# A decoder step on one core: the recorder's rule for a side step of TensorE also looks at the two dense halves behind it

## The chip, the cores and the metric

One core of a Trainium2 chip runs the whole program. The metric is the device time of one execution in microseconds (us); shorter is better. Of the kernel before there are three timed runs and one profiled execution.

## The reference

One layer of a hybrid decoder runs over a prompt of 512 tokens and over 8 samples of 4 tokens each, 544 columns in all, which share the weights (D = 1024, fp32 in and out).

```
z = rmsnorm(x) @ w_in                      # q, k, v of 8 attention heads; q, f, i, gate of 4 HGRN2 heads
att = dilated_attention(q, [cache; k], [cache; v]);  att = head_rmsnorm(att)
f = lb + (1 - lb) * sigmoid(hf)            # HGRN2: S_t = diag(f_t) S_{t-1} + (1 - f_t) outer i_t
o = head_rmsnorm(S_t^T silu(hq)) * silu(hg)
x += [att, o] @ w_out
x += cross_attention(rmsnorm(x), memory_k, memory_v) @ w_co
x += (silu(conv3(rmsnorm(x) @ w_gate)) * (rmsnorm(x) @ w_up)) @ w_down
y = rmsnorm(x)                             # outputs: y, new k and v, HGRN2 states, conv rows, memory k and v
```

## The kernel before

Activations lie transposed in SBUF, 128 features by 544 columns. Each fp32 product of a weight with the activations is made of three products of rounded parts (type fp32r): high by high, high by low, low by high. A **dense half** is one such product for 128 output rows and either 256 or 288 columns: 8 contraction tiles by 3 products, 24 matmuls into one bank of PSUM. In the names, `ps_hf_0` is the half of 256 columns of the projection hf (the forget gate of an HGRN2 head) and `ps_hf_256` the half of 288.

Between the dense halves stands smaller work, mostly in plain fp32, each matmul of which shows in the trace as two records: prompt attention (`psS`, `psT`, `psO`), the samples' attention over the cached window (`psd`, `psdo`), and HGRN2 (`psA`, `psB`, `psL`, `psin`, `psu`, `psU`, `pso`). A step `psdo` multiplies probabilities by a tile `st` of 512 KB of cached values, four matmuls at a time; five such tiles stand in SBUF and SyncE's DMA queue refills each as it comes free. Many matmuls of HGRN2 are only 32 by 32.

The program is not issued as it is written. The class `Tape` records every instruction, joins those of TensorE into steps, and the function `order` then plays the steps through with assumed durations and decides the order on every engine. On TensorE the dense halves are **main** steps in a fixed order. All else there is a **side** step, which may go between two main steps once its inputs are there. When a main step is ready too, a side step must pass two tests: the function `held_back`, which returns how long the step would wait for TensorE's own instructions, must give under 0.1 us, and the array must stay busy enough (`ACTIVE`, `SPELL`). When no main step is ready the tests are not made.

`held_back` and `fetch` carry the recorder's picture of the instruction stream. Instructions come to TensorE in blocks of 256 (`BLOCK`). A variable `codes` counts them. A block counts as asked for when TensorE is 64 instructions short of the end of the block two before it, and as there after 4.3 us (`FETCH`) plus up to 2.2 us for what the DMA queue still holds (`bus`). A matmul of type fp32r counts as 2 instructions and one of fp32 as 4. The other engines' order comes from the same play, so when a TensorE step moves, its inputs' and outputs' instructions and the loads that wait for its buffers move with it.

All instructions of the program that the recorder issues carry one line number, L719 (L691 for DMAs), so the profile is read by the names of tiles.

Of the kernel before, what the change touches and what calls it, by code (L numbers as in the profile page):

```python
# [260 lines left out]
class Tape:  # L261
# [201 lines left out]
    def order(self, before=None):  # L463
# [25 lines left out]
        now, clock, bus, todo, done, burst, first = 0.0, [0.0, 0.0], 0.0, len(self.steps), [], False, None  # L489
# [5 lines left out]
        codes, fetched, heard = self.AHEAD_OF, {0: 0.0, 1: 0.0}, dict.fromkeys(waiting, -1)  # L495

        def hears(s):

            news = {}
            for d in s.deps:  # L500
                if d.engine != "PE" and d.nth > heard[d.engine]:
                    news[d.engine] = max(news.get(d.engine, -1), d.nth)
            return news

        def held_back(s):

            block, wait = (codes + s.codes + len(hears(s)) // 2 - 1) // self.BLOCK, 0.0
            for b in range((codes - 1) // self.BLOCK + 1, block + 1):
                share = (b * self.BLOCK - codes) / s.codes
                at = now + wait + share * s.length  # L510
                wait += max(0.0, fetched.get(b, at + self.FETCH) - at)
            return wait

        def fetch(s, wait):
            nonlocal codes
            news = hears(s)
            codes += len(news) // 2
            heard.update(news)
            for b in range((codes - 1) // self.BLOCK + 1, (codes + s.codes - 1) // self.BLOCK + 1):
                fetched.setdefault(b + 1, now + wait + self.FETCH)  # L520
            for b in range((codes + 63) // self.BLOCK + 1, (codes + s.codes + 63) // self.BLOCK + 1):
                share = max(0.0, (b * self.BLOCK - codes - 64) / s.codes)
                fetched[b + 1] = now + share * (wait + s.length) + self.FETCH + min(2.2, max(0.0, bus - now - 0.5))
            codes += s.codes

        ran, cold, mode = [], [0.0, -10.0], (128, 128)
# [1 line left out]
        def active(at):  # L528

            done = 0.0  # L530
            for a, b, work in reversed(ran):
                if b <= at - self.SPELL:
                    break
                done += work * (b - max(a, at - self.SPELL)) / (b - a)
            return done
# [8 lines left out]
        def fits(s):  # L544
            want = needs(s)
            return all(room[k] >= v for k, v in want.items()) and ("a" not in want or leaves_room(s, want["a"]))
# [18 lines left out]
        def start(s):  # L565
# [9 lines left out]
            if s.bytes:  # L575
                free[s.engine] = now + (0.9 if s.engine == "POOL" else 0.4)
                bus = max(bus, now) + s.bytes / 300e3
                s.end = bus + (3.6 if s.engine == "POOL" else 2.2)
            else:
                held_up = max(0.0, port[s.engine == "DVE"] - now) if s.port else 0.0  # L580
                if s.port:
                    port[s.engine == "POOL"] = now + held_up + s.length
                if s.engine == "PE":
                    held_up = held_back(s) + self.SWITCH * (s.mode != mode)
                    fetch(s, held_up)
                    mode = s.left_in
                    if now > 12.0 and now > cold[1] and active(now) < self.IDLE * self.SPELL:
                        cold[:] = cold[0] + self.COLD, now + 2 * self.SPELL
                    ran.append((now, now + held_up + s.length, s.work))
                free[s.engine] = s.end = now + held_up + s.length  # L590
# [26 lines left out]
        while todo:  # L617
            for f in [f for f in frees if f[0] <= now + 1e-9]:
                room[f[1]] += 1
                frees.remove(f)  # L620
            moved = False
            for e in ("SP", "ACT", "DVE", "POOL"):
                if free[e] <= now + 1e-9:
                    at = clock[0] + min(now - clock[1], 4.0)
                    can = [s for s in waiting[e] if s.ready <= now + 1e-9 and s.begin <= at + (s.lead or self.LEAD) and fits(s)]
                    if can:
                        busy = port[e == "DVE"] > now + 0.1
                        start(min(can, key=lambda s: (s.begin + 2.0 * (s.port and busy), s.number)))
                        moved = True
            if free["PE"] <= now + 1e-9:  # L630
                can = [s for s in waiting["PE"] if s.ready <= now + 1e-9 and fits(s)]
                main = [s for s in can if s.main]
                side = [s for s in can if not s.main]
                if main:
                    side = [s for s in side if held_back(s) < 0.1
                            and active(now + s.length) + s.work >= self.ACTIVE * self.SPELL]
                if side and first is None:
                    first = now
                even = [s for s in side if s.mode == s.left_in == mode == (128, 128)]
                if side and (burst or even or not main or sum(s.length for s in side) >= self.BURST  # L640
                             or now - first > self.PATIENCE
                             or min(s.begin for s in side) < clock[0] + now - clock[1]):
                    s = min(side, key=lambda s: (s.begin + self.NEAR * (s.mode != mode), s.number))
                    if not burst and even and main and sum(s.length for s in side) < self.BURST:
                        s = min(even, key=lambda s: (s.begin, s.number))
                    else:
                        burst, first = True, None
                    start(s)
                    moved = True
                elif main:  # L650
                    start(main[0])
                    if before is not None and now > before[nth[main[0]]] + self.BEHIND:
                        return None
                    burst = False
# [1896 lines left out]
```

## Time and profile before

| what | value |
|---|---|
| three timed runs | 823.06, 824.0 and 825.23 us; the median is 824.0 |
| the profiled execution's own time | 824.86 us |
| its span, first to last instruction | 823.1 us, so 1.76 us lie around it |
| mean granted TensorE clock | 0.993 of full speed |
| VectorE, ScalarE, GpSimd busy | 594.2, 420.8 and 157.0 us |
| bytes moved by DMA | 137.04 MB, 166 GB/s over the span |

The profile names engines by PE (TensorE's matmuls), PEld (its weight loads), DVE (VectorE), ACT (ScalarE), POOL (GpSimd) and SP (SyncE, here only a DMA queue). In the timeline view each row has the start, the time to the end of the last record, the tiles, the part of the array in use (rows*columns), the shape of what is read and how many records were merged. In a view by windows, each row is a stretch of time with the busy time of each engine and its number of instructions, then the granted clock, the busy share of the DMA engines and GB/s. Matmuls overlap in the array, so the pace is read from one start to the next and not from the length of one.

### The profile page before, as it was taken

To read this page: it belongs to the slowest core of one execution; us is meant where nothing else is said; L and a number is where in the kernel's file an instruction comes from. 1 tells how busy PE (TensorE), PEld (TensorE's weight loads), DVE (VectorE), ACT (ScalarE), POOL (GpSimd) and SP (SyncE) were. 2 spreads that over 40 slices of the span, in tenths; PEclk is the share of its full clock that TensorE was granted. 3 is DMA by queue.
4 is the path that set the end of the run, shared out by engine and by line. 5 is a ranking of instruction groups with operands and counts; after the bars stand their busy time and mean duration, and the time that the engine had idled before them with its cause. 6 is when DMAs were issued, how large, how long until landed. Compare 5 with 4: busy or idle time off the path is not lost.

```text
span 823.1 us, 18827 instructions
## 1 busy us (share of the span) xinstructions
PE 809.8 (98%) x7545; PEld 762.9 (93%) x7545; DVE 594.2 (72%) x1252; ACT 420.8 (51%) x838; POOL 157.0 (19%) x246
## 2 busy tenths in 40 slices
PE   9999999989999999999999999999999999999996
PEld 9998988868898879999889999999999999999995
DVE  6775534855778995664579999877677767978983
ACT  8412534514636835453455565654554545666553
POOL 1130000110120220232133351022011212221023
PEclk9999999989999999999999999999999999999999
DMA  9657779676863535253543265556555645776603
GB/s 319 204 143 234 251 228 312 224 252 195 291 190 103 187 105 182 70 147 105 189 157 113 65 172 138 132 150 168 129 129 151 156 135 133 183 186 172 149 3 109
DMA packets 93639, 137.04 MB, mean 166 GB/s; under 512 B 6512, under 2 KB 60656, under 8 KB 93552
## 3 DMA queue, kind: packets, MB, share of 16 engines
q1 hardware_dynamic: 86496, 123.77, 47.2%
q0 software_dynamic: 6336, 11.54, 8.9%
q8 instruction: 59, 0.97, 0.5%
q10 hardware_dynamic: 720, 0.53, 0.2%
q14 instruction: 28, 0.23, 0.1%
HBM read 127.75 MB, written 8.07 MB: 165 GB/s over the span
## 4 chain that ended last, share of the span: by engine, by line
PE 95%; ACT 2%; DMA 1%; DVE 1%; issue 1%; DVEq 0%; ACTq 0%
PE ps_d L719 9%; PE ps_au L719 7%; PE ps_ag L719 7%; PE ps_wo L719 6%; PE ps_cu L719 4%; PE ps_cg L719 3%; PE ps_k L719 3%; PE ps_q L719 3%; PE ps_g L719 3%; PE ps_cq L719 3%; PE ps_first L719 3%; PE ps_dz L719 3%; PE ps_hv L719 3%; PE ps_co L719 3%; PE ps_az L719 2%; PE ps_hf L719 2%
## 5 line engine op out<-in xcount | busy, mean ns | idle before, releaser
L719 ACT CAST wh<-wr 128x1024 fp32r<-128x1024 f32 (+1 forms) x68 | 59.0, 883 | 104.1 <-PE ps_q L719 15.4
L719 DVE TENSOR_TENSOR wl<-wr,wh 128x1024 fp32r<-128x1024 f32 (+1 forms) x68 | 70.9, 1057 | 7.8 <-ACT wh L719 7.5
L719 POOL TENSOR_TENSOR hG<-hG,hf 128x256 f32<-128x256 f32 (+1 forms) x28 | 24.7, 882 | 185.9 <-DVE hf L719 80.6
L719 POOL COPY last<-ug 128x2 f32<-128x2 f32 (+1 forms) x44 | 21.9, 520 | 125.2 <-DVE ug L719 104.6
L719 DVE TENSOR_TENSOR xr<-xr,ps_d 128x256 f32<-128x256 f32 (+1 forms) x48 | 20.9, 436 | 29.7 <-PE ps_d L719 29.5
L719 DVE SCALAR_TENSOR_TENSOR cv<-ug,vec,cv 128x560 f32<-128x560 f32 x44 | 35.1, 799 | 3.6 <-ACT cv L719 3.1
L719 POOL COPY ug<-conv_state 128x16 f32<-128x16 f32 x22 | 20.7, 941 | 17.6 <-PE ps_au L719 9.3
L719 POOL TENSOR_TENSOR acc_cx<-acc_cx,sq_cx 128x256 f32<-128x256 f32 (+1 forms) x14 | 11.7, 838 | 64.2 <-ACT sq_cx L719 64.1
L719 ACT ACTIVATE cv<-cv 128x560 f32<-128x560 f32 x22 | 14.8, 673 | 17.6 <-DVE cv L719 17.6
L719 ACT ACTIVATE P<-P,mx 128x128 f32<-128x128 f32 (+3 forms) x32 | 17.6, 554 | 9.6 <-DVE mx L719 9.5
L719 ACT ACTIVATE cv<-ug,vec 128x560 f32<-128x560 f32 x22 | 18.9, 857 | 4.6 <-DVE ug L719 3.4
L719 PE MATMUL ps_co<-coh,wh 128*128 128x256 f32 (+1 forms) x64 | 19.2, 300 | 0.1
L719 PE MATMUL ps_co<-coh,wl 128*128 128x256 f32 (+1 forms) x64 | 18.4, 288 | 0.0
L719 PE MATMUL ps_co<-col,wh 128*128 128x256 f32 (+1 forms) x64 | 18.4, 288 | 0.0
L691 POOL DMA_DIRECT2D S1u<-in_w_up x10 | 8.8, 879 | 49.6 <-DVE cv L719 25.6
L719 DVE TENSOR_TENSOR xr<-xr,ps_wo 128x256 f32<-128x256 f32 (+1 forms) x16 | 6.8, 435 | 15.5 <-PE ps_wo L719 15.5
L719 DVE TENSOR_TENSOR up<-ps_cu,keptu 128x272 f32<-128x272 f32 x20 | 8.7, 437 | 11.9 <-PE ps_cu L719 11.6
L719 PE MATMUL psdo<-st,dpt 128*32 128x256 f32 x224 | 16.4, 410 | 0.1
L719 PE MATMUL psd<-st,qbd_win 128*32 128x224 f32 x256 | 15.5, 357 | 0.0
L719 POOL TENSOR_TENSOR acc_ux<-acc_ux,sq_ux 128x256 f32<-128x256 f32 (+1 forms) x13 | 11.3, 870 | 20.4 <-ACT sq_ux L719 20.2
L719 DVE TENSOR_TENSOR hf<-ps_hf,r_mix 128x256 f32<-128x256 f32 (+1 forms) x6 | 2.6, 442 | 17.2 <-PE ps_hf L719 17.2
L719 DVE CUSTOM_DVE_ANT_0 P<-psS,bias 128x128 f32<-128x128 f32 (+3 forms) x32 | 14.3, 485 | 1.0 <-PE psS L719 1.0
(2610 smaller groups left out, 3610.5 us busy)
## 6 DMA issues: line engine op xcount, KB each, us to landing
st<-in_kwT SPq DMA_DIRECT2D x32, 448.0 KB, 5.7
st<-in_vw SPq DMA_DIRECT2D x28, 512.0 KB, 6.4
wr<-in_w_in SPq DMA_DIRECT2D x25, 512.0 KB, 4.9
wd<-in_w_down SPq DMA_DIRECT2D x24, 256.0 KB, 3.0
wru<-in_w_up SPq DMA_DIRECT2D x10, 512.0 KB, 5.4
wrg<-in_w_gate SPq DMA_DIRECT2D x9, 512.0 KB, 4.9
st<-in_mkT SPq DMA_DIRECT2D x8, 512.0 KB, 5.7
wr<-in_w_out SPq DMA_DIRECT2D x8, 512.0 KB, 3.6
```

The source lines that it names most:

```text
L691: return tape.put(engine, lambda: call(*args, **kw), outs, ins, 0.1, 0.3, size)
L719: return tape.put(engine, lambda: call(*args, **kw), outs, ins, length, lag, size, port, codes, work, mode)
```

## The change

The recorder's test of a side step becomes a look further ahead. `held_back` takes a number of instructions that follow the step; with 96, which is two dense halves of 48, a side step is held back when the blocks that it and the next two halves need would come too late. The function also works out for each block when it would be asked for, if it has not been asked for yet, and adds the queue of the DMA engines, which until now only `fetch` did.

```
-        def held_back(s):
-
-            block, wait = (codes + s.codes + len(hears(s)) // 2 - 1) // self.BLOCK, 0.0
+        def held_back(s, after=0):
+
+            block, wait = (codes + s.codes + len(hears(s)) // 2 + after - 1) // self.BLOCK, 0.0
             for b in range((codes - 1) // self.BLOCK + 1, block + 1):
-                share = (b * self.BLOCK - codes) / s.codes
+                share = min(1.0, (b * self.BLOCK - codes) / s.codes)
+                asked = now + max(0.0, ((b - 1) * self.BLOCK - 64 - codes) / s.codes) * s.length
                 at = now + wait + share * s.length
-                wait += max(0.0, fetched.get(b, at + self.FETCH) - at)
+                wait += max(0.0, fetched.get(b, asked + self.FETCH + queued()) - at)
             return wait
+
+        def queued():
+            return min(2.2, max(0.0, bus - now - 0.5))
...
                 if main:
-                    side = [s for s in side if held_back(s) < 0.1
+                    side = [s for s in side if held_back(s, 96) < 0.1
                             and active(now + s.length) + s.work >= self.ACTIVE * self.SPELL]
```

`fetch` calls `queued()` in place of the same expression. The same 7,545 matmul records are issued in the same number of instructions; helper lines move down by four (L719 becomes L723, L691 becomes L695). The order on TensorE is the same up to its row 1003 of 5,575 and again from the first halves of `ps_wo`, the output projection, on; between them lies the stretch that took from 162 to 321 us in the trace.

The first place is on TensorE, just ahead of the half `ps_hf_0` of the second HGRN2 head. Before, `psB` and `psA` (products of 32 by 32), a step `psdo` and `pst_v` (transposes of v) stand there:

```order
L719 MATMUL psB_378<-hq_343,hk_375 32x32 x17
L719 MATMUL psB_378<-kq_1_376 32x32 x17
L719 MATMUL psB_378<-kq_2_377 32x32 x17
L719 MATMUL psA_381<-kq_4_379 32x32 x16
L719 MATMUL psdo_429<-st_491,dpt_425 32x256 x4
L719 MATMUL psA_381<-kq_8_380 32x32 x16
L719 MATMUL psS_436<-cs,v_413 32x128
L719 MATMUL pst_v_430<-cs,v_413 128x128 x4
L719 MATMUL ps_hf_0_481<-xm0h,wh_479 128x256
```

On the same engine at the same place, the changed kernel has:

```order
L723 MATMUL psB_378<-hq_343,hk_375 32x32 x17
L723 MATMUL psB_378<-kq_1_376 32x32 x17
L723 MATMUL psB_378<-kq_2_377 32x32 x17
L723 MATMUL psA_381<-kq_4_379 32x32 x16
L723 MATMUL psS_436<-cs,v_413 32x128
L723 MATMUL pst_v_430<-cs,v_413 128x128 x4
L723 MATMUL ps_hf_0_481<-xm0h,wh_479 128x256
```

One step `psdo` (4 matmuls) and the step `psA` of `kq_8` (16 matmuls) have left the place.

The second place is on TensorE at the end of `ps_hf_0`. Before, side steps follow its last matmul, and `ps_hf_256` comes some 60 rows later:

```order
L719 MATMUL ps_hf_0_481<-xm7h,wl_480 128x256
L719 MATMUL psdo_429<-st_492,dpt_427 32x256 x4
L719 MATMUL psdo_429<-st_494,dpt_427 32x256 x4
L719 MATMUL psdo_429<-st_495,dpt_427 32x256 x4
L719 MATMUL psdo_429<-st_501,dpt_427 32x256 x4
L719 MATMUL psA_381<-kq_16_385 32x32 x16
L719 MATMUL psA_381<-cs,hv_362 32x128 x2
L719 MATMUL psdo_429<-st_503,dpt_427 32x256 x4
L719 MATMUL psL_388<-kq_32_386 32x32 x8
```

Now the 24 matmuls of `ps_hf_256` follow `ps_hf_0` at once, and on TensorE the side steps stand behind them:

```order
L723 MATMUL ps_hf_256_484<-xm7h,wl_480 128x288
L723 MATMUL psdo_429<-st_491,dpt_425 32x256 x4
L723 MATMUL psdo_429<-st_492,dpt_427 32x256 x4
L723 MATMUL psdo_429<-st_494,dpt_427 32x256 x4
L723 MATMUL psdo_429<-st_495,dpt_427 32x256 x4
L723 MATMUL psA_381<-kq_8_380 32x32 x16
L723 MATMUL psdo_429<-st_501,dpt_427 32x256 x4
L723 MATMUL psA_381<-kq_16_385 32x32 x16
L723 MATMUL psA_381<-cs,hv_362 32x128 x2
L723 MATMUL psL_388<-kq_32_386 32x32 x8
```

The two steps that left the first place have come here, and the steps on `st_503` and `st_504` stand further back, among `psdt` (transposes), `psin` and `pst_hk`.

The third place is SyncE's DMA queue at that time, which loads value tiles `st`, HGRN2 states `hst` and a weight tile `wr`. Before:

```order
L691 DMA out_vT_out<-v_413 128x544
L691 DMA st_501<-in_vw 128x4x256
L691 DMA st_503<-in_vw 128x4x256
L691 DMA hst_532<-in_s 128x4x128
L691 DMA hst_533<-in_s 128x4x128
L691 DMA wr_556<-in_w_in 128x1024
L691 DMA st_504<-in_vw 128x4x256
```

And on SyncE now:

```order
L695 DMA out_vT_out<-v_413 128x544
L695 DMA st_501<-in_vw 128x4x256
L695 DMA hst_532<-in_s 128x4x128
L695 DMA hst_533<-in_s 128x4x128
L695 DMA wr_556<-in_w_in 128x1024
L695 DMA st_503<-in_vw 128x4x256
L695 DMA st_504<-in_vw 128x4x256
```

The load of `st_503`, which waits for a buffer that a `psdo` step frees, has moved behind the states and the weight tile.

More of the change, by code (lines that the diff above doesn't have):

```diff
@@ L522, in fetch @@
                 share = max(0.0, (b * self.BLOCK - codes - 64) / s.codes)
-                fetched[b + 1] = now + share * (wait + s.length) + self.FETCH + min(2.2, max(0.0, bus - now - 0.5))
+                fetched[b + 1] = now + share * (wait + s.length) + self.FETCH + queued()
             codes += s.codes
```

## Prediction

> **What bounds the kernel now.** I read the first part of the page, then TensorE's waits, then the timeline and the windows around the one long wait, last the DMA queues.
>
> ```profile
> span 823.1 us, 18827 instructions
> PE 809.8 (98%) x7545; PEld 762.9 (93%) x7545; DVE 594.2 (72%) x1252; ACT 420.8 (51%) x838; POOL 157.0 (19%) x246
> q8 instruction: 59, 0.97, 0.5%
> PE ps_hf L719 <- issue: 3.2, 1, 3.2
> PE pst_v L719 <- ACT PT L719: 0.5, 1, 0.5
> ```
>
> TensorE is busy for 809.8 of 823.1 us, so an order of the same matmuls can gain only where TensorE stands or runs slowly. Of its waits one is over 1.1 us: 3.2 us before a matmul of `ps_hf`, with "issue" as releaser, that is, no semaphore that the profile sees. No wait for another engine in the moved stretch is longer than the 0.5 us of the last row. The third row is the instruction queue: 59 transfers, 0.97 MB, 16.4 KB each. TensorE has 2 x 7,545 instructions (matmuls and weight loads), and 15,090 / 59 is 256: one transfer brings 256 instructions, the work of 128 matmul records.
>
> ```profile
> 159.74 1.33 PE L719 MATMUL psdo<-st,dpt 128*32 128x256 f32 x16
> 160.88 0.49 PE L719 MATMUL psB<-hq,hk 128*32 128x32 f32 x33
> 162.13 0.66 PE L719 MATMUL psdo<-st,dpt 128*32 128x256 f32 x8
> 162.57 0.47 PE L719 MATMUL psA<-kq 128*32 128x32 f32 x31
> 162.85 0.29 PE L719 MATMUL psS<-cs,v 128*32 128x128 f32 x1
> 163.59 0.36 PE L719 MATMUL ps_hf<-xm0h,wh 128*128 128x256 f32 x1
> 163.80 0.29 PE L719 MATMUL ps_hf<-xm0l,wh 128*128 128x256 f32 x1
> 164.87 0.28 PE L719 MATMUL ps_hf<-xm3l,wh 128*128 128x256 f32 x1
> 168.37 0.58 PE L719 MATMUL ps_hf<-xm3h,wl 128*128 128x256 f32 x1 [3.23 <-issue]
> 168.75 0.41 PE L719 MATMUL ps_hf<-xm4h,wh 128*128 128x256 f32 x1
> 171.10 0.41 PE L719 MATMUL ps_hf<-xm7h,wl 128*128 128x256 f32 x1
> 171.44 3.16 PE L719 MATMUL psdo<-st,dpt 128*32 128x256 f32 x32
> 174.43 0.46 PE L719 MATMUL psA<-kq 128*32 128x32 f32 x31
> ```
>
> The wait sits in the middle of a half, after its 11th matmul of 24. The inputs were all there for the 10th and 11th, so nothing but the instruction itself is left to be late. Ahead of it stood products of 32 by 32, which use up instructions fast. These windows show how fast, and what the DMA engines and the clock did:
>
> ```profile
> 454.00:470.00 16.00, 16.00 (x130) 16.00 (x130) 15.21 (x32) 9.79 (x13) 6.35 (x10) 1.00 0.32 67
> 161.60:165.10 3.50, 3.50 (x134) 3.05 (x124) 2.80 (x9) 0.84 (x2) 0.71 (x1) 1.00 0.99 331
> 164.80:168.40 3.60, 0.37 (x4) 0.17 (x3) 2.18 (x6) 0.00 (x0) 1.35 (x2) 0.83 1.08 374
> 168.40:174.40 6.00, 6.00 (x45) 4.25 (x49) 2.10 (x5) 0.00 (x0) 0.00 (x0) 0.53 0.74 211
> 174.40:182.40 8.00, 8.00 (x155) 6.82 (x148) 4.79 (x14) 3.15 (x9) 2.11 (x3) 1.00 0.71 243
> ```
>
> In dense work some 130 records last 16 us; just before the wait 134 lasted 3.5 us, with the DMA engines full (0.99). Behind the wait the granted clock is 0.53 up to 174.4, then 1.00 again.
>
> ```profile
> q8 instruction: 1, 0.02, 3.1%
> q8 instruction: 2, 0.03, 0.6%
> q8 instruction: 1, 0.02, 3.0%
> q8 instruction: 1, 0.02, 5.8%
> ```
>
> These are the instruction queue in four windows: 154 to 156 us, 150 to 170, 166 to 168, and 172.2 to 173.3. Between 150 and 170 two blocks moved, one by 156 and one between 166 and 168, while TensorE stood. The next moved from 172.2 on. So some 10 us lie between the first two, and in 3.5 of them TensorE used up a block's 128 records: I take the wait to be for the block of instructions.
>
> **The change, part by part.** First, **what goes**. The wait: 168.37 - 164.87 less one normal step. The normal pace is (164.87 - 163.80) / 9 = 0.119, so 3.38 us. Then the slow clock: from 168.75 to 171.10 eleven steps took 2.35 us where 1.31 is normal, 1.04 lost; the step before them, 0.38, lost 0.26. The 32 records of `psdo` took 174.43 - 171.44 = 2.99; at the 1.14 us for 16 of the row at 159.74 they need 2.28, so 0.71 lost. With 0.1 at the border of the two groups that is 2.1 us, and 5.5 us in all.
>
> Trainium skill, "TensorE: Matmul & The Clock Gate", part 1: it puts the fall to half clock after an idle window of about 3.4 us. Here TensorE stood from 165.15, and a clock of 0.83 over 164.8 to 168.4 means that the half clock began near 167.2, after some 2 us; by the page alone a wait of 2 to 3 us would keep the clock, and the second term would be owed only to how the window lay.
>
> Second, **where the block's edge comes to lie**. The edge is a count, so it can be carried over. Ahead of it the change removes one `psdo` step and the `psA` of `kq_8`: 4 + 16 fp32 matmuls, 40 records. The edge then falls 40 records later: the 13 left of `ps_hf_0`, the 24 of `ps_hf_256`, and 3 of the `psdo` that follows.
>
> ```profile
> 156.60 0.30 PE L719 MATMUL ps_v<-xm0l,wh 128*128 128x288 f32 x1
> 159.51 0.29 PE L719 MATMUL ps_v<-xm7h,wl 128*128 128x288 f32 x1
> ```
>
> A half of 288 goes at 2.91 / 22 = 0.132 a step. The dense work begins at 163.59 less the removed 162.85 - 162.13 = 0.72, so at 162.9; 24 x 0.119, 24 x 0.132, 0.2 for the first steps and 0.2 for three records of `psdo` put the edge at 169.3 to 169.5. The block was usable at 168.37 and nothing that stands ahead of it in the DMA queue has moved. It is there 1 us early: this wait goes.
>
> Third, **the next block**. Its edge lies 128 records on, inside the first products of `psO`. From 169.4 the rows above give 0.07 a record for `psdo`, 0.01 for `psA`, and by the rest of the burst I reach about 173.2. Before, that block moved at 172.2 and the block ahead of it was taken up 1.3 us after its own move ended, at 167.1: usable at about 174.5. Kept so, the wait would be 1.3 us.
>
> ```profile
> 161.46 1.73 SPq L691 DMA_DIRECT2D st<-in_vw  x2
> 163.24 1.87 SPq L691 DMA_DIRECT2D hst<-in_s  x2
> 165.21 2.67 SPq L691 DMA_DIRECT2D wr<-in_w_in  x1
> DMA to landing us min/median/max: 3.4/6.4/8.2
> ```
>
> But the load of `st_503`, the second of these, moves behind `wr`. It has 512 KB, 1.4 us at the 374 GB/s above. If the instruction transfer stands in the line behind these loads, as the two moves (166 and 172.2, the first after 5 us of full DMA engines, the second where they emptied) suggest, it comes 1.4 us earlier, and the block is usable at 173.1: no wait. Bounds 0 and 1.3; I take 0.4, near the shorter end.
>
> Fourth, **what is added**: more changes between shapes of the array. Counted over both orders, with the array part that the timeline gives each tile, neighbours of different shape are 59 before and 70 now in the moved stretch, as `psdt`, `psdo`, `psin`, `psO` and `psL` are cut into smaller pieces.
>
> ```profile
> 62.35 0.55 PE L719 MATMUL psd<-st,qbd_win 128*32 128x224 f32 x6
> 62.91 1.13 PE L719 MATMUL psu<-hvm,hsm 32*128 32x512 f32 x4
> 92.52 0.94 PE L719 MATMUL psd<-st,qbd_win 128*32 128x224 f32 x16
> 93.28 0.24 PE L719 MATMUL psd<-knew,qbd_win 128*32 128x32 f32 x8
> 93.34 0.56 PE L719 MATMUL psd<-st,qbd_win 128*32 128x224 f32 x8
> 93.83 0.39 PE L719 MATMUL ps_k<-xm0h,wh 128*128 128x256 f32 x1
> ```
>
> Sixteen `psd` go in 0.76 us; the eight before the dense half take 0.49 and not 0.38, so 0.11 for that change. Six before `psu` take 0.56 and not 0.29, so up to 0.27. At 0.15, nearer to the row with the dense half, since most of the added ones are like it, 11 changes cost 1.7 us; the bounds are 1.2 and 3.0, and 0 if the array hides them.
>
> Fifth, **what is moved for the others**. On DVE, ACT, POOL and SP the same work is reordered; they are busy 72, 51 and 19% and TensorE is their bottleneck. One place is tighter: the burst of side steps behind `ps_hf_256` now holds some 225 records without a dense half, and `st_503` is loaded only when its first `psdo` frees a buffer, at about 170, for use at 176. That is 6 us; the loads of `st` between 158 and 176 us took 3.4 to 8.2 to land (the last row above). I put 0.3 for waits in that burst, between 0 and 2. The later moves, up to 321 us, shift halves by one or two groups; I cost them at nothing, hidden by a `ps_wo` whose inputs stay two halves ahead, and at 1 us if that cover is gone.
>
> **The sum**: -5.5 + 0.4 + 1.7 + 0.3 = -3.1 us. The profiled execution, 824.86, would become 821.8 and its span 820.0. It lies 0.9 above the median of the timed runs, so from 824.0 I forecast 821.0.
>
> **Rivals.** (a) *The next block comes late and the clock falls again.* Place: the edge near 173.2, in `psO`. It decides when that block is asked for only after the first two `psdo` have freed their buffers, for then two loads of 512 KB, 2.8 us, stand ahead of it, in place of the 1.4 saved: usable at 175.8, a wait of 2.6. That is more than the 2 us after which the clock fell, so the 2.1 us of slow clock come back too: -5.5 + 1.7 + 0.3 + 2.6 + 2.1 = +1.2, 825.2, slower than before. For it: DMA at 1.08 in this stretch. Against it: the block ahead is there at 168.4, before any buffer is freed. (b) *The wait turns into a wait for data in the long burst*, for `st_503` or for `hkt`, which ACT copies between `pst_hk` and `psU`: up to 2 us, 823.0. Against it: TensorE's waits of this kind are at most 0.5 us there now. (c) *The change doesn't do what it says*, because the wait isn't one for instructions: it stays, and the added shape changes make it 825.7. Against it: the transfer in the wait itself. (d) *The shape changes cost nothing*: 818.5 to 819.5.
>
> Trainium skill, "Runtime: NRT & Kernel Launch", section on instruction fetch mechanics: blocks of 16 KiB, 256 instructions, are fetched ahead, and crossing from one to the next is mostly hidden, since issuing is slower than filling. By this rule (c) would hold and nothing would be gained; the trace agrees with the size of the block, but not with the hiding at this place, where 3.23 us are seen.
>
> **How the numbers follow.** Forecast as summed, 0.62, from 818.8 to 822.8; (a) 0.12; (b) 0.14; (c) 0.05; (d) 0.07. About 0.3%, 2.5 us, is what a measurement of this kernel can tell from no change: the border is 821.5, and 826.5 above. Of the forecast's case some 0.43 is below 821.5; with (d) and a little of (b), faster has 0.52. Most of (a), (b) and (c) and the rest of the forecast stay within it: 0.41. Slower has 0.07, for (a) with a longer wait or (c) with dearer changes. The range from 818.6 to 824.2 takes in the forecast, (b) and (d) and leaves out most of (a) and (c).
>
> **What would show it.** The chain of waits, in order of time, has the start of `ps_wo`:
>
> ```profile
> 321.11 48.07 PE ps_wo L719 x384
> ```
>
> In the changed profile TensorE's waits should have no "issue" over 1 us; the clock should be 1.00 in every window between 160 and 180; `ps_hf_256` should start right behind `ps_hf_0` near 166; the instruction queue should move a block near 166 and one near 171; and from 162 us to that start the kernel should be some 3 us shorter. I am wrong in the third step if a new "issue" wait stands in `psO`, in the fourth if that stretch is shorter by 5 us or by less than 2 with no waits in it, and in the fifth if DVE, ACT or a DMA stand among TensorE's waits with over 0.5 us.

## The result, and the profile after

| | before | changed |
|---|---|---|
| timed runs, median (least to most) | 824.24 us (823.06 to 825.23, 6 runs) | 821.08 us (820.59 to 821.92, 6 runs) |
| profiled execution, its span | 824.86, 823.1 us | 821.08, 819.3 us |
| mean granted clock in it | 0.993 | 0.997 |

The ratio is 0.9962, with a 95% interval of 0.995 to 0.9975: faster by 3.2 us. A second comparison, made later, gives less: 822.67 us (15 runs) against 821.25 (11 runs), 0.9981 [0.9972, 0.999]. Both medians of the changed kernel lie in the forecast's range. The second gain, 1.4 us, is less than half of the first; one reason why it can differ is part of what follows.

The page of the changed kernel, its first part, the instruction queue (transfers, MB, share) and the chain by engine:

```profile
span 819.3 us, 18836 instructions
PE 808.6 (99%) x7545; PEld 761.3 (93%) x7545; DVE 594.8 (73%) x1252; ACT 421.3 (51%) x838; POOL 152.9 (19%) x246
q8 instruction: 59, 0.97, 0.5%
PE 95%; ACT 1%; DVE 1%; DMA 1%; SPq 0%; issue 0%; DVEq 0%
```

The list of TensorE's waits in the changed kernel (us in total, times, longest):

```profile
PE ps_first L723 <- DVE zero L723: 1.1, 1, 1.1
PE psT L723 <- ACT PT L723: 0.5, 1, 0.5
PE psr_mix L723 <- DVE acc_mix L723: 0.4, 1, 0.4
PE ps_ck L723 <- DVE v L723: 0.2, 1, 0.2
```

The wait of 3.2 us with "issue" as releaser is gone and no other of its kind has come. `ps_first` waited 1.1 us before too, and `psT`'s 0.5 us stands in place of `pst_v`'s. The 0.4 us of `psr_mix` at the program's start are also in a repeat of the kernel before (the third execution, below); the 0.2 us of `ps_ck` are new. The timeline of the changed kernel at the same place (start, time to the end of the last record, tiles, array part, shape, records):

```profile
165.90 0.28 PE L723 MATMUL ps_hf<-xm7h,wl 128*128 128x256 f32 x1
166.02 0.29 PE L723 MATMUL ps_hf<-xm0h,wh 128*128 128x288 f32 x1
169.07 0.29 PE L723 MATMUL ps_hf<-xm7h,wl 128*128 128x288 f32 x1
169.29 1.94 PE L723 MATMUL psdo<-st,dpt 128*32 128x256 f32 x32
```

The changed kernel by windows (TensorE's busy time and records, its weight loads, VectorE, ScalarE, GpSimd, then granted clock, DMA share, GB/s):

```profile
165.00:168.00 3.00, 3.00 (x25) 3.00 (x25) 1.69 (x5) 0.00 (x0) 0.76 (x2) 1.00 1.08 373
168.00:171.00 3.00, 3.00 (x43) 2.20 (x45) 2.04 (x5) 1.05 (x1) 0.62 (x1) 1.00 0.96 298
171.00:174.00 3.00, 3.00 (x121) 2.69 (x113) 2.71 (x5) 0.77 (x3) 1.03 (x1) 1.00 0.78 231
```

The half of 288 columns follows the half of 256 at 166.02 with no pause, `psdo` starts at 169.29, and the clock is 1.00 throughout while the DMA engines are as full (1.08) as before. The instruction queue in the changed kernel, in the windows 165.5 to 166.6 and 170.3 to 171.5 us:

```profile
q8 instruction: 1, 0.02, 5.4%
q8 instruction: 1, 0.02, 5.7%
```

One block moved in each, where the prediction looked for them (166 and 171).

To see where the rest of the time went, both orders are cut at points by which each has done the same matmuls: the first `psB` of that place, the matmul after which both have issued the same 2,149 records of TensorE, and the first matmul of `ps_wo`. The timeline of before at these points:

```profile
160.88 0.49 PE L719 MATMUL psB<-hq,hk 128*32 128x32 f32 x33
192.57 0.49 PE L719 MATMUL psS<-k,q 64*128 64x128 f32 x4
320.95 0.28 PE L719 MATMUL ps_wo<-om0h,wh 128*128 128x256 f32 x1
```

The timeline of the changed kernel at the same points:

```profile
161.12 0.49 PE L723 MATMUL psB<-hq,hk 128*32 128x32 f32 x32
187.32 0.38 PE L723 MATMUL ps_hq<-xm0h,wh 128*128 128x288 f32 x1
316.95 0.28 PE L723 MATMUL ps_wo<-om0h,wh 128*128 128x256 f32 x1
```

The first part fell from 31.69 to 26.20 us, by 5.49. The second grew from 128.38 to 129.63, by 1.25. The start ahead of `psB` took 0.24 longer and the stretch from `ps_wo` to the end 0.22 (823.09 - 320.95 = 502.14 against 819.31 - 316.95 = 502.36): 3.8 us in all, the difference of the spans. The 0.24 are no effect of the change: TensorE's order is the same up to there, and `psB` starts at 160.71 and 161.29 us in two more executions of before, at 161.74 in a second one of the changed kernel. The 0.22 are there in these executions too (502.12 and 502.15 against 502.31); their cause is open.

### The profile page after: what moved, and what is told of

Read it like the earlier page. It is cut to its first block, busy times and chain, and to the rows that moved or that the text cites. A ratio compares the mean times of both kernels' runs of the same rounds, so it can differ in the third digit from the quotient of the medians.

```text
span 819.3 us, 18836 instructions
## 1 busy us (share of the span) xinstructions
PE 808.6 (99%) x7545; PEld 761.3 (93%) x7545; DVE 594.8 (73%) x1252; ACT 421.3 (51%) x838; POOL 152.9 (19%) x246
## 4 chain that ended last, share of the span: by engine, by line
PE 95%; ACT 1%; DVE 1%; DMA 1%; SPq 0%; issue 0%; DVEq 0%
PE ps_d L723 9%; PE ps_au L723 7%; PE ps_ag L723 7%; PE ps_wo L723 6%; PE ps_cu L723 4%; PE ps_cg L723 3%; PE ps_k L723 3%; PE ps_q L723 3%; PE ps_hv L723 3%; PE ps_g L723 3%; PE ps_cq L723 3%; PE ps_v L723 3%; PE ps_dz L723 3%; PE ps_co L723 3%; PE ps_az L723 2%; PE ps_hq L723 2%
## 5 line engine op out<-in xcount | busy, mean ns | idle before, releaser
L723 ACT CAST wh<-wr 128x1024 fp32r<-128x1024 f32 (+1 forms) x68 | 59.4, 883 | 100.9 <-PE ps_q L723 15.4
L723 DVE TENSOR_TENSOR wl<-wr,wh 128x1024 fp32r<-128x1024 f32 (+1 forms) x68 | 71.6, 1062 | 8.3 <-ACT wh L723 7.7
L723 POOL TENSOR_TENSOR hG<-hG,hf 128x256 f32<-128x256 f32 (+1 forms) x28 | 24.4, 870 | 185.6 <-DVE hf L723 86.5
L723 POOL COPY last<-ug 128x2 f32<-128x2 f32 (+1 forms) x44 | 21.0, 500 | 128.0 <-DVE ug L723 107.3
L723 DVE TENSOR_TENSOR xr<-xr,ps_d 128x256 f32<-128x256 f32 (+1 forms) x48 | 20.9, 436 | 29.9 <-PE ps_d L723 29.8
L723 DVE SCALAR_TENSOR_TENSOR cv<-ug,vec,cv 128x560 f32<-128x560 f32 x44 | 35.1, 798 | 3.7 <-ACT cv L723 3.1
L723 ACT ACTIVATE cv<-cv 128x560 f32<-128x560 f32 x22 | 14.8, 673 | 17.8 <-DVE cv L723 17.7
L723 POOL TENSOR_TENSOR acc_cx<-acc_cx,sq_cx 128x256 f32<-128x256 f32 (+1 forms) x14 | 11.7, 837 | 58.5 <-ACT sq_cx L723 58.4
L723 ACT ACTIVATE P<-P,mx 128x128 f32<-128x128 f32 (+3 forms) x32 | 17.6, 553 | 9.1 <-DVE mx L723 8.9
L723 ACT ACTIVATE cv<-ug,vec 128x560 f32<-128x560 f32 x22 | 18.8, 857 | 4.2 <-DVE ug L723 3.2
L723 POOL COPY ug<-conv_state 128x16 f32<-128x16 f32 x22 | 17.3, 787 | 15.4 <-PE ps_au L723 9.1
L723 PE MATMUL ps_co<-coh,wh 128*128 128x256 f32 (+1 forms) x64 | 19.2, 300 | 0.1
L723 DVE TENSOR_TENSOR xr<-xr,ps_wo 128x256 f32<-128x256 f32 (+1 forms) x16 | 6.8, 436 | 16.3 <-PE ps_wo L723 16.3
L723 PE MATMUL ps_co<-col,wh 128*128 128x256 f32 (+1 forms) x64 | 18.4, 288 | 0.0
L695 POOL DMA_DIRECT2D S1u<-in_w_up x10 | 8.8, 877 | 51.7 <-DVE cv L723 26.2
L723 PE MATMUL ps_co<-coh,wl 128*128 128x256 f32 (+1 forms) x64 | 18.4, 288 | 0.0
L723 DVE TENSOR_TENSOR up<-ps_cu,keptu 128x272 f32<-128x272 f32 x20 | 8.7, 437 | 11.5 <-PE ps_cu L723 11.2
L723 PE MATMUL psd<-st,qbd_win 128*32 128x224 f32 x256 | 15.5, 358 | 0.0
L723 DVE CUSTOM_DVE_ANT_0 P<-psS,bias 128x128 f32<-128x128 f32 (+3 forms) x32 | 14.3, 485 | 1.2 <-PE psS L723 1.2
L723 POOL TENSOR_TENSOR acc_ux<-acc_ux,sq_ux 128x256 f32<-128x256 f32 (+1 forms) x13 | 11.3, 871 | 20.3 <-ACT sq_ux L723 20.1
L723 PE MATMUL psdo<-st,dpt 128*32 128x256 f32 x224 | 14.8, 385 | 0.0
```

What stands on the lines that cost most here:

```text
L695: return tape.put(engine, lambda: call(*args, **kw), outs, ins, 0.1, 0.3, size)
L723: return tape.put(engine, lambda: call(*args, **kw), outs, ins, length, lag, size, port, codes, work, mode)
```

## The experiments

**Is the wait one for a block of instructions?** Theory: the edge of a block is a count of instructions, so instructions added at the program's start, which the recorder's play doesn't see, move the edge to other work while the order stays. Rival: the wait belongs to the matmul or its data. `hidden` makes the recorder issue an instruction at once and leave it out of its play; the added fp32 products of 128 by 2 (two records each) stand in the warm-up of TensorE and their results are not used. In the first run 48 of them, 96 records:

```
+            tape.hidden = True
+            warm_up(48, 2)
+            tape.hidden = False
```

> The order of before, word for word, with 48 more tiny fp32 products (128x2, zeros, overwritten later) in the warm-up at the program's start: 96 records more stand ahead of everything, so every edge between blocks of 256 instructions falls 96 records earlier. Nothing else is changed, and the planner doesn't see them. Theory (the wait of 3.2 us in ps_hf is for a block of instructions): it leaves the middle of ps_hf. The edge goes from record 1875 to 1779, into psB, where its block was asked for in the dense half before, and the next edge to record 1907, into the psdo behind ps_hf_0. No issue wait in ps_hf; one of at most 1 us in psdo and one of up to 2 us near psO; no half clock at 168 to 174 us; from the first psB of that place to the first ps_wo 155 to 158 us (160.1 before, 155.8 in the changed kernel). Rival 1 (the wait is for data or for a bank of PSUM that ps_hf needs): it stays where it is, 3.2 us ahead of ps_hf<-xm3h,wl, and the stretch stays 160. Rival 2 (the gain of the change is due to its order as such): the stretch stays 160, since the order is that of before.

The kernel took 840.13 us, some 17 more than the kernel before; most of the added products ran at half clock, which the trace shows from 8.03 to 25.10 us. There is no wait in `ps_hf` any more. The timeline shows where the largest one now is:

```profile
190.06 0.93 PE L721 MATMUL psO<-PT,vt 128*64 128x128 f32 x11
192.63 0.43 PE L721 MATMUL psO<-PT,vt 128*64 128x128 f32 x3 [1.65 <-issue]
```

Counted from the program's first matmul, before's wait stood ahead of record 1875. Here waits of 0.2 us stand ahead of record 1875, which now is in `psB`, and of record 2003 (`psdo`), and this one stands ahead of 2130: the same count, one block further and two, all at other matmuls. From the first `psB` to `ps_wo` it took 157.69 us, where before took 160.07. The rival, by which `ps_hf` waits whatever the count, falls.

With 16 products, 32 records, in the order of before:

> The order of before with 16 tiny products more in the warm-up, so that every edge falls 32 records earlier: from record 1875 to 1843, just ahead of the dense half ps_hf_0, while its block was asked for at nearly the same time as before. Theory: the wait moves ahead of ps_hf_0 (into psA, psS or pst_v) and grows from 3.2 to 4.5 to 5.5 us, since 11 dense matmuls and some small ones no longer stand before it; the clock halves behind it as before; from the first psB to the first ps_wo 161 to 163 us. Rival 1 (data or a bank): the wait stays at 3.2 us inside ps_hf. Rival 2 (the place of the edge doesn't matter): no difference from before.

```profile
166.04 0.35 PE L721 MATMUL psA<-kq 128*32 128x32 f32 x17
169.84 0.30 PE L721 MATMUL psA<-kq 128*32 128x32 f32 x12 [3.45 <-issue]
```

The wait moved 32 records up the order, into the `psA` ahead of the half, and stands at record 1875 again. It is shorter than the expected 4.5 to 5.5 us, and the clock stayed at 1.00 there although TensorE stood longer than in the profiled execution of before; the stretch took 157.61 us and not 161 to 163. So the wait is shown to be for instructions, and the half clock isn't its certain companion; the second miss led to the runs on the clock below. This kernel took 825.87 us.

What ends such a wait can be read as well. All traces of this study together have ten waits with issue as releaser, and each of them ends 1.30 to 1.45 us after a block's move on the instruction queue has ended (in the kernel before: moved by 167.06, next matmul at 168.37).

With 20 products, 40 records, in the changed order:

> The order of the changed kernel with 20 tiny products more in the warm-up: every edge falls 40 records earlier, from record 1875 to 1835, in the psA ahead of ps_hf_0. Theory: the changed order is good for its own count alone, so the wait comes back, 3 to 4 us, ahead of ps_hf_0, with the half clock behind it, and from the first psB to the first ps_wo it takes 160 to 162 us (155.8 in the changed kernel). Rival 2 (the order as such is faster, wherever the edges fall): no issue wait over 1 us there, and the stretch stays 156.

The wait came back, ahead of record 1875 and of the same matmul `xm3h,wl` of `ps_hf_0` as before. The expectation had the right shift and named the wrong place, `psA`: the change took 40 records away ahead of this matmul and the products add 40. The kernel's list of waits has:

```profile
PE ps_hf L725 <- issue: 1.1, 1, 1.1
```

It is 1.1 us and not 3 to 4, the clock stayed at 1.00, and from `psB` to `ps_wo` it took 157.20 us where the changed kernel takes 155.83: 1.37 more, about the wait. The kernel took 830.27 us. The place followed the count each time; in the last two runs the length of the wait was over-estimated.

**Which of the two edits does it?** The new reckoning of when a block is asked for, alone, leaves the order of TensorE's rows as it was. So the look ahead was run alone, with the old reckoning:

```
-        def held_back(s):
+        def held_back(s, after=0):
-            block, wait = (codes + s.codes + len(hears(s)) // 2 - 1) // self.BLOCK, 0.0
+            block, wait = (codes + s.codes + len(hears(s)) // 2 + after - 1) // self.BLOCK, 0.0
-                    side = [s for s in side if held_back(s) < 0.1
+                    side = [s for s in side if held_back(s, 96) < 0.1
```

> One part of the change alone: the look ahead over 96 instructions, without the new time at which a block not yet asked for would come. The order on TensorE is that of the changed kernel up to about 280 us of the trace and differs in 56 lines behind it, where block 27 of the instructions has 3.9 us from its being asked for to its edge, against 8.4 in the changed kernel and 4.9 before. Theory: the wait in ps_hf is gone as in the changed kernel, so the first part carries the gain: 821 to 822.5 us; the second edit is worth 0 to 1 us, by a wait for instructions of up to 1 us near 290 us. Rival (the second edit carries the gain): 823.5 to 825 us.

821.78 us (10 runs) against 823.58 (13 runs), 0.9978 [0.9968, 0.9989]; no issue wait, not near 290 us either, and 156.67 us from `psB` to `ps_wo` against 155.83, with a wait of 0.5 us of `psU` for ScalarE that the changed kernel doesn't have. The look ahead brings the gain; whether the other edit adds to it is within what can be told apart.

**How far should it look?** One half (48) and three halves (144) in place of two:

```
-                    side = [s for s in side if held_back(s, 96) < 0.1
+                    side = [s for s in side if held_back(s, 48) < 0.1
```

> The change with a look ahead of 48 instructions, one dense half in place of two. The order differs from the changed kernel in 70 lines of TensorE's rows, with 3 changes of shape fewer; the edge of the block that was late falls into the middle of ps_hf_256, needed at about 169 us where it was usable at 168.4 before. Theory (only the room before an edge and the changes of shape count): the wait is gone here too; block 27 near 289 us has only 3.9 us, which costs 0 to 1 us; 820.3 to 822 us. Rival (the long look is needed): a wait for instructions of over 1 us comes back at 165 to 175 us, 822.5 us or more.

> The change with a look ahead of 144 instructions, three dense halves. The order differs from the changed kernel in 200 lines; as many changes of shape (72). Theory: no wait near 165 us; the tightest place is block 22 near 237 us, 5.4 us from asked to needed, against 6.7 before: a wait of up to 1 us there; 820.5 to 822.5 us. Rival (a longer look is better throughout): under 820.3 us.

With 48: 822.05 us against 823.11, 0.9984 [0.9974, 0.9993]. A wait remains one edge further on, at record 2002; the theory had none, the rival one of over 1 us:

```profile
172.31 0.57 PE L723 MATMUL psL<-kq 128*32 128x32 f32 x14
173.78 0.22 PE L723 MATMUL psL<-kq 128*32 128x32 f32 x2 [0.90 <-issue]
```

With 144: 821.3 us, 0.9978 [0.9968, 0.9987], no issue wait (up to 1 us was expected), 156.32 us from `psB` to `ps_wo`. The intervals of 48, 96 and 144 overlap; the traces tell only that 48 leaves 0.9 us of waiting.

**What does a change of the array's shape cost?** Tiny products, fp32, 128 by 2, were put ahead of halves of three projections (`wo`, `cq`, `co`); the half overwrites their result. In the first kernel they use the array as the halves do (128*128), in the second 128*32, which makes two changes of shape around each. The lines of the second:

```
+            if name[:2] in ("wo", "cq", "co"):
+                tape.hidden = True
+                nc.tensor.matmul(ps[:32, :2], C("ones")[:, :32], C("ones")[:, :2], start=True, stop=True)
+                tape.hidden = False
```

> The changed kernel with one tiny fp32 product more (128 rows by 128 columns of the array, 2 columns of data, overwritten by what follows) ahead of each of 37 dense halves of ps_wo, ps_cq and ps_co. It changes nothing of the shapes and is there to be compared with the next run. Both theories: the stretch of those halves becomes longer by what 37 such products cost, 2 to 14 us (by the 48 of the first experiment, 0.36 us each at half clock).

> The same 37 tiny products, but in 128 rows by 32 columns of the array, so that almost each brings two changes of shape, some 70 in all. Theory (a change of shape costs 0.15 us, as the prediction priced it): longer than the run before by 8 to 13 us over that stretch. Rival (a change costs little, and what the changed order lost of its gain is something else): longer by under 4 us, 0.05 a change.

`ps_wo` in the chain of waits of the first of the two (start, length):

```profile
318.53 51.00 PE ps_wo L725 x410
```

The same row of the second:

```profile
317.81 52.68 PE ps_wo L725 x410
```

And the added records of the second, from its groups by line (shortest, median and longest in ns, first and last start, array part):

```profile
L725 PE MATMUL ps_wo<-cs x26: 171/182/192, 326.3 to 366.9; 128*32 128x2 f32 x26
```

The 26 records are 13 products, with 26 changes of shape around them. They cost 52.68 - 51.00 = 1.68 us more, which is 0.065 us a change if the product itself takes equally long in both shapes. Over all three projections it is 4.71 us: the theory's 8 to 13 are not reached, the rival's 4 are passed. Both kernels took more time for the added work (830.2 and 834.13 us), of which only their difference counts here.

That the product takes equally long is not shown, and the rows speak against it. At 128*32, 31 records of `psA` go in 0.28 us (from 162.57 to 162.85 in the prediction's timeline), 0.01 each, while the product at 128*128 costs 0.22 us ((51.00 - 48.15) / 13, the second from the changed kernel's row at the end of this text). The product at 128*32 costs 0.35 with its two changes ((52.68 - 48.15) / 13). If its two records take 0.02 of that, some 0.16 us are left for each change, which is an estimate. So the runs put the price of a change between 0.065 and some 0.16 us and do not settle it.

**Does the half clock follow from the wait?** The kernel before, twice more unchanged, each in a profiled execution of its own:

> The kernel before, unchanged, in one more profiled execution, for the question whether the half clock belongs to the wait. Theory (the wait belongs to the program, the clock term doesn't): a wait with issue as releaser of 2.5 to 4 us again in ps_hf, its gap ahead of record 1875 of TensorE's stream; the granted clock behind it may be half for some us or stay at 1.00. From the start of the first psB of that place to the first matmul of ps_wo: 160.1 us where the clock falls, 158.0 where it doesn't. Rival (the clock falls after each such wait, and the run with 32 records more was an exception): half clock again, 160 us.

> The same once more, with the same two expectations: the wait at record 1875 by both; by the theory a stretch near 158.0 us with the clock at 1.00 or near 160.1 with half clock, by the rival always 160.

The timeline of the first of them, at the wait and at the two later cuts:

```profile
167.64 0.39 PE L719 MATMUL ps_hf<-xm3h,wl 128*128 128x256 f32 x1 [2.09 <-issue]
189.48 0.49 PE L719 MATMUL psS<-k,q 64*128 64x128 f32 x4
317.87 0.28 PE L719 MATMUL ps_wo<-om0h,wh 128*128 128x256 f32 x1
```

The timeline of the second at the same points:

```profile
167.01 0.38 PE L719 MATMUL ps_hf<-xm3h,wl 128*128 128x256 f32 x1 [1.99 <-issue]
190.23 0.38 PE L719 MATMUL psS<-k,q 64*128 64x128 f32 x2
318.88 0.28 PE L719 MATMUL ps_wo<-om0h,wh 128*128 128x256 f32 x1
```

The wait stood at record 1875 in both and was only some 2 us long (2.5 to 4 were expected). The first execution kept the clock at 1.00 and took 156.58 us from `psB` (161.29) to `ps_wo`; the second fell to half clock and took 158.18 (from 160.71). The expected 158.0 and 160.1 were both too long, mostly by the shorter wait; in the second, also, one window ran at half clock and not two. The wait belongs to the program, the half clock to the execution.

What decides it can be read in part. All changes of the clock in these traces lie on a grid of 3.41 us. These are windows on that grid, in the profiled execution of before:

```profile
163.74:167.15 3.41, 1.41 (x12) 1.20 (x11) 2.33 (x8) 0.59 (x1) 1.39 (x2) 1.00 1.07 378
167.15:170.57 3.42, 2.20 (x10) 2.20 (x11) 0.35 (x2) 0.00 (x0) 0.67 (x1) 0.50 1.14 341
170.57:173.98 3.41, 3.41 (x29) 1.84 (x32) 2.10 (x5) 0.00 (x0) 0.00 (x0) 0.50 0.45 133
```

The windows of the first repeat:

```profile
163.63:167.04 3.41, 1.92 (x16) 1.72 (x15) 2.34 (x8) 0.84 (x2) 1.39 (x2) 1.00 1.08 368
167.04:170.45 3.41, 2.81 (x33) 2.28 (x37) 1.83 (x6) 0.00 (x0) 0.67 (x1) 1.00 1.16 333
```

The windows of the second repeat:

```profile
164.89:168.30 3.41, 1.42 (x13) 1.29 (x12) 2.01 (x6) 0.00 (x0) 1.35 (x2) 1.00 1.07 358
168.30:171.71 3.41, 3.41 (x33) 1.81 (x35) 2.10 (x5) 0.00 (x0) 0.00 (x0) 0.50 1.02 299
```

The windows of the kernel with 32 records more, around its wait:

```profile
164.81:168.22 3.41, 1.58 (x129) 1.37 (x120) 2.93 (x8) 0.00 (x0) 0.60 (x1) 1.00 1.11 352
168.22:171.63 3.41, 1.79 (x29) 1.59 (x30) 2.19 (x6) 0.84 (x2) 1.44 (x3) 1.00 1.08 367
```

Where TensorE was busy for 1.41 or 1.42 us of a window, the next window runs at half clock; where it was busy for 1.58 to 1.92, the clock stays. In the last kernel the longest stand, 3.45 us, fell across two windows, and neither was empty enough. In the second repeat the clock even falls at 168.30, over 1 us after the wait had ended. The ends of all the traces agree with it: behind a window with 0 to 1.20 us of work the clock falls, behind one with 1.91 us or more it doesn't. That how a stand lies on the grid decides is read from these executions; it was not tested by moving a stand along the grid on purpose. The Trainium skill, "TensorE: Matmul & The Clock Gate", part 1, says that the window is 3.4 us long and free-running, so that where a transition comes varies from run to run. The traces agree with that; the fall after a window with 1.4 us of work is not in its rule of an idle window.

Busy time alone isn't what decides, though. The kernel with 96 records more has these two windows on its grid, in which TensorE does nothing but the added products of two columns:

```profile
4.62:8.03 3.41, 3.41 (x33) 3.41 (x32) 2.13 (x4) 1.68 (x3) 0.55 (x1) 1.00 1.01 335
8.03:11.44 3.41, 3.41 (x19) 3.41 (x18) 2.21 (x5) 3.28 (x7) 0.00 (x0) 0.50 1.03 381
```

The records fill the first window and the clock falls all the same; in the kernel with 32 records more it does so at 7.79 us. So the figures of 1.4 and 1.6 us hold for the work that stands around this wait.

The changed kernel was run again beside them:

> The changed kernel again, timed beside the kernel before on this chip, with a second profile. Theory: no issue wait over 0.3 us and no half clock between 6 and 814 us, the stretch from psB to ps_wo at 155.8 to 156.3 us, the time 821.0 to 821.5, and a ratio of 0.996 to 0.998, since the clock term is there in only some executions of the kernel before. Rival (the wait's 3.4 us and the clock's 2.1 are both there in every execution of the kernel before): ratio of 0.9945 to 0.9955.

821.25 us against 822.67, 0.9981 [0.9972, 0.999], just outside the expected ratios; no issue wait over 0.3 us, no half clock between 6 and 814 us, 156.16 us from `psB` to `ps_wo`. The kernel before ran 64 times in the four later comparisons. Its mean granted clock was 0.995 or less in 41 of these executions, with a median of 823.64 us, and 0.997 or more in 14, with 822.13. Of 17 timed executions of the changed kernel none was below 0.996; their median is 821.11. So by this split the kernel before is only some 1.0 us behind the changed one without its half clock, and 2.5 with it. In the second comparison 8 of its 15 executions were at 0.995 or less, beside the version of the next experiment 15 of 17, and its gain is 2.4 us. For the first comparison the clock is on record for one execution of before alone, so that why it gives 3.2 us is argued and not shown.

**Is what is given back beyond 187 us owed to the order there?** The look ahead was switched off behind the place of the wait (`codes` is the recorder's count of instructions):

```
-                    side = [s for s in side if held_back(s, 96) < 0.1
+                    side = [s for s in side if held_back(s, 96 if codes < 4200 else 0) < 0.1
```

> The changed rule up to the place of the wait and the old one behind it: TensorE's order is the changed kernel's up to the half ahead of the second psB group (near 215 us) and the one of before from there on. Theory (the changed order gains the whole wait and clock at the first place, and gives back some 1.1 us beyond 219 us, where its order is only worse): no issue wait over 0.3 us; from record 1817 to record 2150 25.0 us as in the changed kernel, from record 2426 to record 3900 134.6 us as in the kernel before and not 135.7; psB to ps_wo near 154.8 us, span near 818.4, time near 820.2, ratio 0.995 to 0.998. Rival (what is given back comes from the earlier start of the later work, whatever its order: loads and other engines have as much less time): 135.2 to 135.7 us in the later part and 821.0 to 821.5.

821.38 us (12 runs) against 823.79 (17 runs), 0.9969 [0.9959, 0.9979], not told apart from the changed kernel. From record 1817 to 2150 it took 24.96 us, as expected; from 2426 to 3900 135.77. This (0.07 above its range) and the time fit the rival and not the theory, but the timeline shows another cause:

```profile
226.74 0.27 PE L723 MATMUL psS<-cs,v 128*32 128x128 f32 x1
228.00 0.30 PE L723 MATMUL psS<-cs,v 128*32 128x128 f32 x1 [0.99 <-issue]
```

A new wait for instructions, 1.26 us from start to start, stands ahead of record 2637, six blocks behind the first. Past it the old order has its old speed: from record 2802 to 3900 it took 113.27 us, the kernel before 113.27 and the changed one 114.28. By the rival this part would be slower too, since it starts at 239.99 us, 4.43 earlier than before (244.42). So the theory on the order holds behind record 2802, and the later part of the changed order isn't only worse: it costs 1.0 us there, and it has no wait of 1.2 us where this version has one. The two nearly cancel, and no version that was run beats the change.

## Why the prediction was right

The forecast was 821.0 us, the medians 821.08 and 821.25. Point by point:

- **What goes.** 5.5 us were forecast, 3.38 for the wait and 2.1 for the slow clock. The first part of the stretch fell by 5.49. Against the repeat without half clock (161.29 to 189.48, 28.19 us, gap 2.37) the profiled execution of before took 3.50 more: 1.14 by its longer gap, and so 2.36 by the clock. So for this execution the first term was right and the second 0.26 too small. As terms of the kernel both were too large: the wait less one step is 2.25 and 2.15 us in the two repeats, and the clock term is owed only in executions where the clock falls. The prediction took both from one execution as if they were always there. That execution had two half-clock windows and the longest of the three waits seen in profiles of this kernel, so its own gain, 3.8 us, is more than the median's.
- **The edge.** Forecast at 169.3 to 169.5, three records into `psdo`; `psdo` starts at 169.29 and runs through. The count that carries the edge over was right, and the runs with added records show that it is a count.
- **The next block.** 0.4 us was forecast, between 0 and 1.3. It is 0: the block moves at 170.3 to 171.5, as the shorter line of loads gave it. There was little room: record 2002 goes 1.57 us after the end of that move, where the waits of this study ended 1.30 to 1.45 us after one. That the move of the one load did it was not tried by itself. Rival (a) did not happen; rival (c) falls with the first three runs.
- **Changes of the array's shape.** 11 at 0.15 made 1.7 us. The prediction read the price from neighbours of unlike work in the first 100 us, where the step from one product to the next also differs in length. The runs with tiny products put it between 0.065 and some 0.16. All that was added in the stretch is 0.26 + 1.25 = 1.51 us, at most 0.14 a change if nothing else became cheaper; in its first part, with 14 neighbours of different shape in the trace against 9, it is 0.26 for five changes. So the term is rather too large than too small, and its true size stays open. Rival (d), no cost at all, is wrong too.
- **What is moved for the others.** 0.3 us of waits in the long side burst: none came there, so rival (b) did not happen either. At the first place all that was added comes to 26.20 - (28.19 - 2.25) = 0.26 us, 2.25 being the gap of 2.37 less one step. Instead the later moves, which the prediction costed at nothing, gave back 1.25 us between 187 and 317 us. Six added changes of shape can explain 0.4 to 1.0 of it by the bounds above, `ps_ck`'s wait for VectorE 0.2. Cut at further points where both orders have done the same work, the difference lies in pieces from -0.5 to +0.4 us, and what each is owed to stays open.

In sum: forecast -5.5 + 0.4 + 1.7 + 0.3 = -3.1; measured in the profiled executions -3.39 - 2.36 + 0.26 + 1.25, that is, -4.24, and with the 0.46 at the program's two ends -3.8. The terms added were put at 2.4 and came to 2.0, in other places; the terms that go were put at 5.5 and came to 5.75.

The mechanism was right: the wait is for a block, the count carries its edge over, and dense work ahead of the edge removes the wait. That the time is met so closely is in part luck. The gain depends on which executions of before stand beside the changed kernel: it is 3.2 us in the first comparison, near the 3.0 forecast, and 1.4 in the second, less than half of it. Against the first repeat of before, with its wait of 2.09 us and full clock, the stretch from `psB` to `ps_wo` is only 0.75 us shorter (156.58 to 155.83).

The rule of the Trainium skill, "Runtime: NRT & Kernel Launch", section on instruction fetch mechanics, that a crossing from block to block is mostly hidden, holds for nearly all of the 59 blocks here; it fails where some 130 records go in 3.5 us while the DMA engines are full, with waits of up to 3.5 us. That the full DMA engines are what makes the block late was not tried by itself.

## What to carry to other kernels

A wait on TensorE that no semaphore explains, behind a run of very small matmuls and beside full DMA engines, may be one for instructions: count records from the program's start, and see whether the place stays at the same count when some records are added ahead. Such a wait is removed by putting dense work ahead of the edge, but the next edges must be looked at too, since time won ahead brings them closer to their blocks. Before a gain is sized from one profiled execution, its half-clock windows should be set apart, and a second execution looked at.

## What the runs showed of the hardware

- The granted clock changed only on a grid of 3.41 us: around this wait 1.4 us of work in a window brought half clock in the next, 1.6 us did not. Products of two columns brought it even where their records filled the window. One window at half clock cost some 1.4 us here (29.52 - 28.19 us in the first part, with a wait shorter by 0.11), two cost 2.4.
- The wait for one and the same block lasted 1.99, 2.09 and 3.23 us in three executions of the same program; ten waits for blocks each ended 1.30 to 1.45 us after the end of a move on the instruction queue.
- The edges lie 127 or 128 matmul records apart (1875, 2002 or 2003, 2130, 2637), where 256 instructions would be 128; other instructions of TensorE, of which the traces show some, can take the missing places.
- A change of the array's part between a half and a tiny product cost between 0.065 and some 0.16 us (the upper end an estimate), and an fp32 product of 128 by 2 some 0.22 us at full clock ((51.00 - 48.15) / 13, the second from this row of the changed kernel's chain):

```profile
317.12 48.15 PE ps_wo L723 x384
```
